# Recurrence of a hybrid decoder layer: products of two heads together, PSUM copies on VectorE, the fourth gate in another bank

## The chip, the cores and the metric

The kernel runs on one core of a Trainium2 chip. The metric is the device time of one execution in microseconds (us); the lower the better. The kernel before takes 1249.21 us, the median of three runs (1248.67 to 1249.44).

## What is computed

The reference is one decoder layer over 512 tokens of width 1024, in float32: a SwiGLU block, then two token mixers side by side (dilated attention, and a gated linear recurrence), a gated merge of the two, an output product, and a second SwiGLU block, with norms between. The change touches the recurrence and the merge gates. Cut to what matters:

```python
xc = causal_conv_width4(xr) + conv_b                       # xr = u @ w_in[:, xr columns]
gate_x = sigmoid(xh @ w_x + b_x); gate_a = sigmoid(xh @ w_a + b_a)   # per head of 256 channels, 4 heads
log_a = -8 * gate_a * softplus(-a_param)
h[t]  = exp(log_a)[t] * h[t-1] + sqrt(1 - exp(2*log_a))[t] * (gate_x * xc)[t]
rec   = h * gelu(yr)                                       # yr = u @ w_in[:, yr columns]
merged = sigmoid(gl0) * attn_d + sigmoid(gl1) * (rec @ w_rec_branch)  # gl = u @ w_in[:, gl columns]
```

## The kernel before, in words

Activations lie with channels on the 128 partitions and the 512 tokens along the free axis. A float32 product is made of three TensorE products of rounded parts: every operand is split into a high part (a ScalarE copy, line 263) and a low part (a VectorE subtraction, line 264), and `mm3` (lines 275 to 278) adds high by high, high by low and low by high into one PSUM bank. A product of one 128-channel block with the whole width (`gemm`, line 291) is thus 8 times 3 = 24 matmuls. The PSUM's eight banks are given out in two rings: `acc_ps` (line 266) with five banks, for the large products, and `aux_ps` (line 269) with three.

Weights arrive in one stream in the order of `stream_plan` (line 67), two blocks of 1024 columns to a load, into two raw buffers; `fetch` (line 223) splits a block into one of four `w8` buffers. The order in which an engine works is fixed when the program is built: a scheduler takes the instructions in the order of the Python text, except that `tc.high_priority(offset=...)` moves some of them ahead of it, a weight split by `AHEAD` = 100 places and a copy out of PSUM by `EVAC` = 200. What is not ready by the scheduler's own reckoning is passed over for what is. On the chip each engine then works through its list in that fixed order.

The recurrence (lines 981 to 1105) has four heads, `hd` = 0 to 3, of two channel blocks each. Its parts are:

- `conv(hd)`, line 1019: two products with `um`; ScalarE copies each PSUM result, with its tokens put in another order, into `xr` (line 1027); ScalarE and three VectorE steps make the convolution (lines 1029 to 1032) into a tile called `sig`; the result is split into `rec.hi` and `rec.lo` (line 1033).
- `branch(hd)`, line 1035: two products with `um`, each copied out by VectorE (line 1043) into a tile `ge`, of which there are four.
- `gates_of(hd)`, line 1047: four gate products of 6 matmuls each on the convolution's result, in four PSUM tiles that all come from the three banks of `aux_ps` (line 1054); ScalarE evacuates each with a sigmoid (line 1060) into a `gt` tile, of which there are six.
- `recur(hd)`, line 1064: some 14 ScalarE and 18 VectorE steps over the two blocks: tanh, exponential, square root and GELU on ScalarE (lines 1071 to 1086), products and the scan over time on VectorE (lines 1076 to 1091), and a split into `rec` at the end (line 1092). Its work tiles `th` and `r0` come from a ring of four.
- the merge gate of the recurrence: one product with `um` per block, and a sigmoid out of PSUM by ScalarE into `sig[:, c, :]` (line 1104). `GATE1` says which blocks stand behind which head: none behind head 0, two behind heads 1 and 2, four behind head 3.

The order before is: conv 0; then for each head branch(hd), conv(hd+1), gates and recurrence of hd, merge gates of `GATE1[hd]`. Behind it stands the product with `w_rec_branch` (line 1110), eight blocks whose 24 matmuls take `rec` block by block, so that the two blocks of head 3 are needed last. Each result is multiplied with the merge gate (line 1111).

Of the kernel before, what the change touches and what calls it, by code (L numbers as in the profile page):

```python
# [10 lines left out]
F32 = mybir.dt.float32  # L11
F32R = mybir.dt.float32r
AF = mybir.ActivationFunctionType
# [3 lines left out]
P = 128  # L17
T = 512
# [6 lines left out]
NH = 4  # L25
# [5 lines left out]
EVAC = 200  # L31
# [3 lines left out]
QKB = 6  # L35
CB = 6
GATE1 = ((), (0, 1), (2, 3), (4, 5, 6, 7))

# [26 lines left out]
def stream_plan():  # L67

    plan = []

    def down(n, a, half):
        for kk in range(part_blocks(a)):
            plan.append((("down", n, a, half, kk), 1024))

    def ffn(n):
        for ev in ffn_order(n):
            if ev[0] == "std":
                plan.append((("gate", n, ev[1]), 1024))
                plan.append((("up", n, ev[1]), 1024))
            elif ev[0] == "prep":  # L80
                plan.append((("gu", n, ev[1]), 2048))
            elif ev[0] == "down":
                down(n, *ev[1:])
            else:
                for half in ev[3]:
                    down(n, ev[2], half)
        for half in range(2):
            down(n, len(FF_PARTS) - 1, half)

    def values(g):  # L90
        for k in range(4):
            plan.append((("v", g, k), 1024))

    def qk(h):
        for g in range(NG):
            plan.append((("pair", g * 4 + h, 12 + g * 4 + h), 2048))

    ffn(1)
    del plan[:4]
    for k in range(KC):  # L100
        plan.insert(k, (("start", k), 512))
    for g in VALUES:
        values(g)
    for h in range(NH):
        qk(h)
    for c in range(0, KC, 2):
        plan.append((("pair", 52 + c, 53 + c), 2048))
    for m in range(KC):
        plan.append((("attn", m), 512))
    for h in range(-1, NH):  # L110
        if h >= 0:
            for c in (2 * h, 2 * h + 1):
                plan.append((("in", 44 + c), 1024))
        if h + 1 < NH:
            for c in (2 * h + 2, 2 * h + 3):
                plan.append((("in", 36 + c), 1024))
        if h < 0:
            continue
        plan.append((("lru", h), 1024))
        for c in GATE1[h]:  # L120
            plan.append((("in", 60 + c), 1024))
    for m in range(KC):
        plan.append((("rec", m), 1024))
    for half in range(2):
        for kk in range(4):
            plan.append((("out", half, kk), 1024))
    ffn(2)
    return plan
# [25 lines left out]
def hybrid_layer(ctx: ExitStack, tc: tile.TileContext, xT: bass.AP, xN: bass.AP, wst: bass.AP,  # L154
                 small: bass.AP, rows: bass.AP, consts: bass.AP, bias: bass.AP, out: bass.AP):
    nc = tc.nc
    DVE, ACT, PE = nc.vector, nc.scalar, nc.tensor
# [65 lines left out]
    def fetch(key, slot=None, ahead=0):  # L223

        with tc.high_priority(offset=ahead if slot else AHEAD):
            src = raw_of(key)
            w = src.shape[-1]
            t = slot() if slot else w8() if w > 512 else w4()
            split(t[:, 0, :w], t[:, 1, :w], src)
            return t[:, 0, :w], t[:, 1, :w]  # L230
# [35 lines left out]
    def acc_ps():  # L266
        return psum.tile([P, T], F32, name="acc", tag="acc", bufs=5)

    def aux_ps():
        return psum.tile([P, T], F32, name="aux", tag="aux", bufs=3)  # L270
# [20 lines left out]
    def gemm(ps, wt, x, sl=slice(0, T), n=None):  # L291
        n = n or x.n
        a, b = k128(wt[0], n), k128(wt[1], n)
        for k in range(n):
            mm3(ps, a[:, k, :], b[:, k, :], x.hi[k][:, sl], x.lo[k][:, sl], k == 0, k == n - 1)
# [446 lines left out]
    um = act_of(um_t[:2], um_t[2:])  # L742
# [12 lines left out]
    with ExitStack() as mx:  # L755
# [220 lines left out]
        for c in range(KC):  # L976
            ps = acc_ps()
# [3 lines left out]
    with ExitStack() as mx:  # L981
# [3 lines left out]
        sig = rpool.tile([P, KC, T], F32, name="sig")  # L985
        lpool_cm = tc.tile_pool(name="lru", bufs=1)
        lpool = lpool_cm.__enter__()
# [4 lines left out]
        o, w = SMALL["ap"]  # L992
# [20 lines left out]
        def ip(ap):  # L1013
            return ap.rearrange("q (i p) -> q p i", p=4)

        def pi(ap):
            return ap.rearrange("q (p i) -> q p i", p=4)

        def conv(hd):

            for c in (2 * hd, 2 * hd + 1):
                ps = acc_ps()
                gemm(ps, fetch(("in", 36 + c)), um)
                xr = lpool.tile([P, 3 + T], F32, name="xr", tag="xr", bufs=2)
                DVE.memset(xr[:, 0:3], 0.0)
                with tc.high_priority(offset=EVAC):
                    ACT.activation(ip(xr[:, 3:]), pi(ps), AF.Copy)
                xc = sig[:, c, :]
                ACT.activation(xc, xr[:, 3:], AF.Identity, bias=col("cb", c), scale=col("cw", 3 * 8 + c))
                for t in (2, 1, 0):  # L1030
                    DVE.scalar_tensor_tensor(xc, xr[:, t:t + T], col("cw", t * 8 + c), xc,
                                             op0=ALU.mult, op1=ALU.add)
                split(rec.hi[c], rec.lo[c], xc)

        def branch(hd):

            gel = []
            for c in (2 * hd, 2 * hd + 1):
                ps = acc_ps()
                gemm(ps, fetch(("in", 44 + c)), um)  # L1040
                ge = lpool.tile([P, T], F32, name="ge", tag="ge", bufs=4)
                with tc.high_priority(offset=EVAC):
                    DVE.tensor_copy(ge, ps)
                gel.append(ge)
            return gel

        def gates_of(hd):
            wh, wl = fetch(("lru", hd))
            a_ = wh.rearrange("p (w i c) -> p w i c", w=2, i=2)
            b_ = wl.rearrange("p (w i c) -> p w i c", w=2, i=2)  # L1050
            gs = {}
            for w, bn in ((1, "ba"), (0, "bx")):
                for j in range(2):
                    ps = aux_ps()
                    for i in range(2):
                        js = slice(j * P, (j + 1) * P)
                        mm3(ps, a_[:, w, i, js], b_[:, w, i, js], rec.hi[2 * hd + i], rec.lo[2 * hd + i],
                            i == 0, i == 1)
                    g = lpool.tile([P, T], F32, name="gt", tag="gt", bufs=6)
                    ACT.activation(g, ps, AF.Sigmoid, bias=col(bn, 2 * hd + j))  # L1060
                    gs[w, j] = g
            return [gs[1, j] for j in range(2)], [gs[0, j] for j in range(2)]

        def recur(hd, gel, gas, gxs):

            cs = (2 * hd, 2 * hd + 1)
            ths, rs = [tmp("th") for _ in cs], [tmp("r0") for _ in cs]
            for c, th, ga in zip(cs, ths, gas):  # L1070
                ACT.activation(th, ga, AF.Tanh, scale=sp4[:, c:c + 1])
            for c, r0, ga in zip(cs, rs, gas):
                ACT.activation(r0, ga, AF.Exp, scale=sp8[:, c:c + 1])
            for r0, th, ga in zip(rs, ths, gas):
                ACT.activation(r0, r0, AF.Copy, bias=0.5, scale=0.5)
                DVE.scalar_tensor_tensor(ga, th, 1.0, r0, op0=ALU.add, op1=ALU.mult)
                DVE.scalar_tensor_tensor(r0, ga, 2.0, r0, op0=ALU.subtract, op1=ALU.mult)
                DVE.tensor_mul(ga, th, r0)
            for c, gx in zip(cs, gxs):
                DVE.tensor_mul(gx, gx, sig[:, c, :])  # L1080
            for th in ths:
                ACT.activation(th, th, AF.Sqrt)
            for ga in gas:
                ACT.activation(ga, ga, AF.Copy, bias=1.0, scale=2.0)
            for ge in gel:
                ACT.activation(ge, ge, AF.Gelu_apprx_tanh)
            for c, r0, th, ga, gx, ge in zip(cs, rs, ths, gas, gxs, gel):
                DVE.scalar_tensor_tensor(th, th, -2.0, r0, op0=ALU.mult, op1=ALU.mult)
                DVE.tensor_mul(gx, gx, th)
                DVE.tensor_tensor_scan(th, ga, gx, 0.0, op0=ALU.mult, op1=ALU.add)  # L1090
                DVE.tensor_mul(pi(ge), ip(th), pi(ge))
                split(rec.hi[c], rec.lo[c], ge)

        conv(0)
        for hd in range(NH):
            gel = branch(hd)
            if hd + 1 < NH:
                conv(hd + 1)
            gas, gxs = gates_of(hd)
            recur(hd, gel, gas, gxs)  # L1100
            for c in GATE1[hd]:
                ps = acc_ps()
                gemm(ps, fetch(("in", 60 + c)), um)
                ACT.activation(sig[:, c, :], ps, AF.Sigmoid)
        lpool_cm.__exit__(None, None, None)

        mg = act_big("mg")
        for c in range(KC):
            ps = acc_ps()
# [145 lines left out]
```

## Time and profile before

| | |
|---|---|
| median of three runs | 1249.21 us |
| the profiled execution | 1251.04 us |
| its span | 1249.3 us |
| recurrence, from its first product to the first product with `w_rec_branch` | 645.2 to 802.1 us of the span |
| load of one 1024 KB pair of weight blocks, issue to landing | 4.8 us |

The profiled execution's span is what the engines' records cover; the rest of its time lies around it. In the rows below, PE is TensorE, PEld its weight loads, DVE VectorE, ACT ScalarE and SP the queue that issues the weight loads. A row of the timeline has the start and the length in microseconds, the engine, the line, the operation, what it writes and reads, and in brackets how long the engine stood idle before it and what it waited for. Neighbouring instructions of one kind are merged into a row, with their count. A matmul's row is longer (0.39 us) than the distance to the next one, because matmuls overlap.

### The profile page before, as it was taken

Reading aid. Unit: us, or ns where it says so; the run is one execution under the profiler, and the core shown is the slowest. Engines: PE = TensorE matmul, PEld = TensorE weight load, DVE = VectorE, ACT = ScalarE, POOL = GpSimd, SP = SyncE. Lnnn points to the kernel's source line nnn. Section 1 sums busy time; section 2 is a strip of 40 time slices with the busy share of each in tenths; the row PEclk is TensorE's granted clock in tenths of the full one; section 3 lists DMA queues with packets and bytes.
Section 4 is the critical chain, followed back from the end, with each engine's and each line's share of the span. In section 5 each row is a group of like instructions: output and inputs, shape, how many; then the busy total and the mean of one; then the engine's idle time right before and its main releaser. Section 6 shows DMA issues by size and latency. Waiting matters only on the chain.

```text
span 1249.3 us, 18949 instructions
## 1 busy us (share of the span) xinstructions
PE 1235.0 (99%) x7712; PEld 1117.5 (89%) x7712; DVE 911.3 (73%) x1427; ACT 670.5 (54%) x1105; POOL 26.1 (2%) x51
## 2 busy tenths in 40 slices
PE   9999999999999999999999999999999999999997
PEld 7899999999878899999987787888899999999985
DVE  6996777786577588888565877754795867777755
ACT  6655444455355365666546979634564544445432
POOL 0000000000002000000000000000100000000000
PEclk9999999999999999999999999999999999999999
DMA  6212222234424222222342122224451322222241
GB/s 241 102 68 102 102 102 103 103 133 171 172 97 144 87 91 102 77 97 82 111 160 102 68 101 102 101 101 168 135 169 68 136 102 102 102 102 74 103 178 67
DMA packets 27527, 141.37 MB, mean 113 GB/s; under 512 B 3120, under 2 KB 6320, under 8 KB 13360
## 3 DMA queue, kind: packets, MB, share of 16 engines
q1 hardware_dynamic: 20160, 122.86, 27.3%
q0 software_dynamic: 7280, 17.30, 4.1%
q8 instruction: 60, 0.98, 0.3%
q14 instruction: 27, 0.22, 0.1%
HBM read 129.67 MB, written 6.29 MB: 109 GB/s over the span
## 4 chain that ended last, share of the span: by engine, by line
PE 90%; DVE 5%; ACT 4%; DMA 1%; issue 1%; SPq 0%; DVEq 0%; ACTq 0%
PE acc L585 11%; PE acc L586 11%; PE acc L587 11%; PE acc L381 7%; PE acc L382 7%; PE acc L380 7%; PE acc L276 7%; PE acc L278 7%; PE acc L277 7%; PE aux L585 3%; PE aux L586 3%; PE aux L587 3%; PE acc L784 1%; PE acc L786 1%; PE acc L785 1%; DVE w L264 1%
## 5 line engine op out<-in xcount | busy, mean ns | idle before, releaser
L264 DVE TENSOR_TENSOR w<-raw,w 128x1024 fp32r<-128x1024 f32 (+1 forms) x241 | 257.9, 1074 | 115.8 <-ACT w L263 84.8
L263 ACT ACTIVATE w<-raw 128x1024 fp32r<-128x1024 f32 (+1 forms) x241 | 225.3, 938 | 181.5 <-DVE raw L566 60.4
L585 PE MATMUL acc<-big,w 128*128 128x256 f32 x880 | 251.2, 285 | 0.1
L586 PE MATMUL acc<-big,w 128*128 128x256 f32 x880 | 250.2, 284 | 0.0
L587 PE MATMUL acc<-big,w 128*128 128x256 f32 x880 | 249.9, 284 | 0.0
L585 PEld LDWEIGHTS acc<-big,w 128*128 128x128 f32 x880 | 168.7, 192 | 1.2 <-ACT c L592 0.3
L586 PEld LDWEIGHTS acc<-big,w 128*128 128x128 f32 x880 | 168.9, 192 | 0.6
L587 PEld LDWEIGHTS acc<-big,w 128*128 128x128 f32 x880 | 168.8, 192 | 0.0
L592 ACT ACTIVATE c<-acc 128x256 f32<-128x256 f32 x169 | 63.9, 378 | 79.7 <-PE acc L587 76.1
L380 PE MATMUL acc<-wd,act 128*128 128x512 f32 x256 | 99.9, 390 | 0.0
L381 PE MATMUL acc<-wd,act 128*128 128x512 f32 x256 | 99.9, 390 | 0.0
L382 PE MATMUL acc<-wd,act 128*128 128x512 f32 x256 | 99.5, 390 | 0.0
L585 PE MATMUL aux<-big,w 128*128 128x256 f32 x280 | 79.4, 283 | 0.0
L586 PE MATMUL aux<-big,w 128*128 128x256 f32 x280 | 79.3, 283 | 0.0
L587 PE MATMUL aux<-big,w 128*128 128x256 f32 x280 | 79.3, 283 | 0.0
L585 PE MATMUL acc<-tx,w 128*128 128x256 f32 x268 | 76.2, 284 | 0.0
L586 PE MATMUL acc<-tx,w 128*128 128x256 f32 x268 | 76.0, 283 | 0.0
L587 PE MATMUL acc<-tx,w 128*128 128x256 f32 x268 | 75.9, 283 | 0.0
L276 PE MATMUL acc<-big,w 128*128 128x512 f32 x192 | 74.8, 389 | 0.0
L278 PE MATMUL acc<-big,w 128*128 128x512 f32 x192 | 74.8, 389 | 0.0
L277 PE MATMUL acc<-big,w 128*128 128x512 f32 x192 | 74.8, 389 | 0.0
L264 DVE TENSOR_TENSOR w<-s,w 128x1024 fp32r<-128x1024 f32 x51 | 62.4, 1224 | 10.4 <-ACT w L263 10.3
(309 smaller groups left out, 2763.5 us busy)
## 6 DMA issues: line engine op xcount, KB each, us to landing
raw<-in_w SPq DMA_DIRECT2D x110, 1024.0 KB, 4.8
big<-act POOLq DMA_DIRECT2D x6, 512.0 KB, 4.3
gains<-in_rows POOLq DMA_DIRECT2D x5, 512.0 KB, 4.9
raw<-in_w SPq DMA_DIRECT2D x8, 256.0 KB, 5.1
h<-in_x SPq DMA_DIRECT2D x8, 256.0 KB, 5.2
h<-in_xn POOLq DMA_DIRECT2D x4, 512.0 KB, 7.2
kept_m<-h POOLq DMA_DIRECT2D x4, 512.0 KB, 2.9
h<-kept_m POOLq DMA_DIRECT2D x4, 512.0 KB, 5.9
```

What stands on the lines that cost most here:

```text
L263: ACT.activation(dh, src, AF.Copy)
L264: DVE.tensor_sub(dl, src, dh.bitcast(F32))
L276: PE.matmul(ps, wh, xh, start=first, stop=False)
L277: PE.matmul(ps, wh, xl, start=False, stop=False)
L278: PE.matmul(ps, wl, xh, start=False, stop=last)
L380: PE.matmul(ps, x.hi[k][:, bl], wh, start=k == 0, stop=False)
L381: PE.matmul(ps, x.hi[k][:, bl], wl, start=False, stop=False)
L382: PE.matmul(ps, x.lo[k][:, bl], wh, start=False, stop=k == x.n - 1)
L585: PE.matmul(ps, wh, xh, start=start and k == 0, stop=False, skip_group_check=True)
L586: PE.matmul(ps, wh, xl, start=False, stop=False, skip_group_check=True)
L587: PE.matmul(ps, wl, xh, start=False, stop=k == 3, skip_group_check=True)
L592: ACT.activation(c, ps, AF.Copy)
```

## The change

A hand-written order, `LRU_ORDER`, takes the place of the loop over heads, for the weight stream as for the program:

conv 0, branch 0, branch 1, conv 1, gates 0, conv 2, gates 1, merge gates of head 1, branch 2, branch 3, conv 3, gates 2, merge gates of head 2, gates 3, merge gates of head 3.

Here "gates" stands for the gate products and the recurrence behind them. Within it:

```diff
-                    ACT.activation(ip(xr[:, 3:]), pi(ps), AF.Copy)
+                    DVE.tensor_copy(ip(xr[:, 3:]), pi(ps))
...
-                ge = lpool.tile([P, T], F32, name="ge", tag="ge", bufs=4)
+                ge = lpool.tile([P, T], F32, name="ge", tag="ge", bufs=8)
...
+        def gelus(hds):
+            for hd in hds:
+                for ge in gels[hd]:
+                    ACT.activation(ge, ge, AF.Gelu_apprx_tanh)
+
+        def sigmoids():
+
+            while late:
+                c = late.pop(0)
+                ACT.activation(sig[:, c, :], sig[:, c, :], AF.Sigmoid)
+
+        def gate1(hd):
+            for c in GATE1[hd]:
+                ps = acc_ps()
+                gemm(ps, fetch(("in", 60 + c)), um)
+                with tc.high_priority(offset=EVAC):
+                    DVE.tensor_copy(sig[:, c, :], ps)
+                late.append(c)
...
+            sigmoids()
             for w, bn in ((1, "ba"), (0, "bx")):
                 for j in range(2):
-                    ps = aux_ps()
+                    ps = aux_ps() if w or not j else acc_ps()
...
-            for ge in gel:
-                ACT.activation(ge, ge, AF.Gelu_apprx_tanh)
...
+        for what, hd in LRU_ORDER:
+            if what == "gates":
+                recur(hd, gels.pop(hd), *gates_of(hd))
+            else:
+                {"conv": conv, "branch": branch, "gate1": gate1}[what](hd)
+                if what == "branch" and hd % 2:
+                    gelus((hd - 1, hd))
+        sigmoids()
```

So the four GELUs of two heads stand together behind their branch products; the convolution's input and the merge gates are copied out of PSUM by VectorE; the merge gates' sigmoids stand, on the copied tile, ahead of the next head's gate sigmoids, and those of head 3 at the very end; and the fourth gate product of each head goes to one of the five banks of `acc_ps`.

More of the change, by code (lines that the diff above doesn't have):

```diff
@@ L37 @@
 GATE1 = ((), (0, 1), (2, 3), (4, 5, 6, 7))
+LRU_ORDER = (("conv", 0), ("branch", 0), ("branch", 1), ("conv", 1), ("gates", 0), ("conv", 2), ("gates", 1),
+             ("gate1", 1), ("branch", 2), ("branch", 3), ("conv", 3), ("gates", 2), ("gate1", 2), ("gates", 3),
+             ("gate1", 3))
 def ffn_order(n):
@@ L109, in stream_plan @@
         plan.append((("attn", m), 512))
[L110 to L121, printed above, removed]
+    for what, h in LRU_ORDER:
+        if what == "gates":
+            plan.append((("lru", h), 1024))
+        else:
+            cs = GATE1[h] if what == "gate1" else (2 * h, 2 * h + 1)
+            o = {"conv": 36, "branch": 44, "gate1": 60}[what]
+            for c in cs:
+                plan.append((("in", o + c), 1024))
     for m in range(KC):
@@ L1033, in conv @@
                 split(rec.hi[c], rec.lo[c], xc)
+        gels, late = {}, []
         def branch(hd):
-            gel = []
+            gels[hd] = []
             for c in (2 * hd, 2 * hd + 1):
@@ L1040, in branch @@
                 gemm(ps, fetch(("in", 44 + c)), um)
-                ge = lpool.tile([P, T], F32, name="ge", tag="ge", bufs=4)
+                ge = lpool.tile([P, T], F32, name="ge", tag="ge", bufs=8)
                 with tc.high_priority(offset=EVAC):
                     DVE.tensor_copy(ge, ps)
-                gel.append(ge)
-            return gel
+                gels[hd].append(ge)
+        def gelus(hds):
[13 more added lines that the diff above has]
+                late.append(c)
         def gates_of(hd):
@@ L1092, in recur @@
                 split(rec.hi[c], rec.lo[c], ge)
[L1094 to L1104, printed above, removed]
+        for what, hd in LRU_ORDER:
+            if what == "gates":
+                recur(hd, gels.pop(hd), *gates_of(hd))
+            else:
+                {"conv": conv, "branch": branch, "gate1": gate1}[what](hd)
+                if what == "branch" and hd % 2:
+                    gelus((hd - 1, hd))
+        sigmoids()
         lpool_cm.__exit__(None, None, None)
```

## Prediction

> **What bounds the kernel now.** I first read the page for the engine that never rests.
>
> ```profile
> span 1249.3 us, 18949 instructions
> PE 1235.0 (99%) x7712; PEld 1117.5 (89%) x7712; DVE 911.3 (73%) x1427; ACT 670.5 (54%) x1105; POOL 26.1 (2%) x51
> ```
>
> TensorE is busy for 99% of the span; its whole idle time is 14 us. A change elsewhere gains only by closing a hole in its row. So the second view is the recurrence by itself, and the third the waits in it.
>
> ```profile
> 645.20:802.10 156.90, 153.67 (x674) 125.89 (x674) 114.99 (x148) 122.33 (x155) 0.00 (x0) 1.00 0.28 99
> ```
>
> ```profile
> PE aux L276 <- ACT gt L1060: 3.2, 4, 1.5
> DVE ge L1043 <- PE acc L278: 5.2, 2, 3.1
> ACT w L263 <- DMA raw<-in_w: 4.5, 1, 4.5
> ```
>
> The columns of the first are span, then busy time of PE, PEld, DVE, ACT. In 156.90 us TensorE is idle for 3.2 (156.90 less 153.67), and the waits name one cause: four times it stands before a gate product until a gate sigmoid (line 1060) is done. The granted clock is 1.00. Weights from memory made ScalarE wait once, at the stage's start, and TensorE never. The timeline shows each wait.
>
> ```profile
> 682.19 0.39 PE L277 MATMUL acc<-big,w 128*128 128x512 f32 x1
> 683.33 0.50 PE L276 MATMUL aux<-rec,w 128*128 128x512 f32 x1 [0.75 <-ACT gt L1060]
> ...
> 710.90 0.39 PE L276 MATMUL acc<-big,w 128*128 128x512 f32 x1
> 712.82 0.51 PE L276 MATMUL aux<-rec,w 128*128 128x512 f32 x1 [1.54 <-ACT gt L1060]
> ...
> 750.40 0.39 PE L277 MATMUL acc<-big,w 128*128 128x512 f32 x1
> 751.54 0.50 PE L276 MATMUL aux<-rec,w 128*128 128x512 f32 x1 [0.76 <-ACT gt L1060]
> ...
> 778.24 0.39 PE L278 MATMUL aux<-rec,w 128*128 128x512 f32 x1
> 778.80 0.50 PE L276 MATMUL aux<-rec,w 128*128 128x512 f32 x1 [0.18 <-ACT gt L1060]
> ```
>
> It is the same matmul each time, the first of a head's fourth gate product: three banks, four tiles, and the fourth has to wait until the first is read. The reader is late because of what ScalarE has in front of it; for head 2:
>
> ```profile
> 746.85 1.08 ACT L1027 ACTIVATE xr<-acc 128x512 f32<-128x512 f32 x1
> ...
> 749.51 1.28 ACT L1060 ACT_TABLE_LOAD   x1
> 750.80 1.27 ACT L1060 ACTIVATE gt<-aux,sm 128x512 f32<-128x512 f32 x2
> ```
>
> A copy from PSUM, two more steps and a table load come first. The sigmoid starts at 750.80, and TensorE goes on at 751.54, when the first of the two has ended. The gate products themselves had begun at 746.09:
>
> ```profile
> 746.09 0.39 PE L276 MATMUL aux<-rec,w 128*128 128x512 f32 x1
> ...
> 749.94 0.39 PE L278 MATMUL aux<-rec,w 128*128 128x512 f32 x1
> ```
>
> These are the 18 matmuls of three gates, 3.85 us from first to last start: a matmul every 3.85 / 17 = 0.227 us.
>
> **The change, part by part.**
>
> *Fourth gate in another bank.* Start to start, the four stalls are 1.14, 1.92, 1.14 and 0.56 us, so over the pitch of 0.227 0.91 + 1.69 + 0.91 + 0.33 = 3.84 us. The stalled matmul itself is longer than the others, 0.50 for 0.39, which I take as 0.11 more, four times 0.44. Sum: **4.3 us** that TensorE loses in the stage, and the most that this edit can return. I take all of it: the new bank is one of five, and the tile five products earlier was copied out long ago, a product being 24 times 0.227 = 5.44 us. Its own reader may come late, since it is next needed five products, some 27 us, further on. What this adds is therefore nothing; if that cover is gone the gain is (below).
>
> *Is anything else late at TensorE in the new order?* Gates need a convolution that is split. The convolution products that ended where head 2's gates began, at 746.09, were split by 753.97:
>
> ```profile
> 753.29 0.68 DVE L264 TENSOR_TENSOR rec<-sig,rec 128x512 fp32r<-128x512 f32 x1
> ```
>
> That is 7.9 us. In the new order the closest pairs, conv 1 to gates 1 and conv 3 to gates 3, have a gates part (5.44) and two products (10.88) between them, 16.3 us. It costs nothing. The weight loads keep number and size, 28 blocks in the stage in pairs; only their order changes, so the waiting row above is my bound for SP's queue: zero.
>
> *Copies moved to VectorE, table loads saved.*
>
> ```profile
> L1027 ACT ACTIVATE xr<-acc 128x512 f32<-128x512 f32 x8 | 8.7, 1086 | 12.0 <-PE acc L278 12.0
> L1091 DVE TENSOR_TENSOR ge<-th,ge 128x512 f32<-128x512 f32 x8 | 8.5, 1070 | 0.0
> L1104 ACT ACT_TABLE_LOAD x6 | 7.7, 1283 | 0.1
> L1043 DVE COPY ge<-acc 128x512 f32<-128x512 f32 x8 | 5.5, 682 | 5.2 <-PE acc L278 5.2
> L1104 ACT ACTIVATE sig<-acc 128x512 f32<-128x512 f32 x8 | 4.8, 595 | 0.1
> ```
>
> VectorE gains eight merge-gate copies at 0.68 (the row of line 1043 is the same copy), 5.5 us, and eight copies with reordered tokens. These no row shows; the straight copy's 0.68 and ScalarE's 1.09 for the same views bound them. I take 1.07, as line 1091, which reads the same reordered view: 8.6 us. VectorE goes from 115.0 to 129 of then 152.6 us. ScalarE loses 8.7 us of copies, and most of the six table loads of line 1104 (7.7 us), and some for GELU; the sigmoids stay. All of it lies beside TensorE, except at the end of the stage.
>
> *The tail, where it is tight.* Before, a branch pair (10.9 us) stood between gates 2 and gates 3. It has gone to the front, so both last recurrences must end sooner: rec is read right behind the last merge gate. Let T be the start of gates 2. Gates 2, two products, gates 3, four products make 8 x 5.44 = 43.5 us; block 7's low part is wanted at the 23rd matmul behind, at T + 43.5 + 22 x 0.227 = **T + 48.5**. From before:
>
> ```profile
> 770.34 1.08 DVE L1091 TENSOR_TENSOR ge<-th,ge 128x512 f32<-128x512 f32 x1
> ...
> 784.91 0.69 DVE L1076 SCALAR_TENSOR_TENSOR gt<-th,r 128x512 f32<-128x512 f32 x1 [2.48 <-ACT r L1075]
> ...
> 800.79 0.68 DVE L264 TENSOR_TENSOR rec<-ge,rec 128x512 fp32r<-128x512 f32 x1
> ```
>
> ```profile
> 780.40 0.72 ACT L1071 ACTIVATE th<-gt,sp 128x512 f32<-128x512 f32 x1
> ```
>
> Head 2 frees its second `th` tile 771.42 - 746.09 = 25.3 us after its gates start, and head 3's second tanh wants that tile. From that tanh to head 3's first product before: 784.91 - 780.40 = 4.5. From there to the last split: 801.47 - 784.91 = 16.6, VectorE without a hole. To this come some three merge-gate copies, 3 x 0.60 (copies follow each other closer than their length) = 1.8. Sum T + 48.2. Head 2's first sigmoid came 4.7 us after its gates' start (750.80 - 746.09), 1.1 of them ScalarE's xr copy, which goes: T + 47.1. **To spare: 1.4 us.** Before it was 5.6: the low part was ready at 801.47, its matmul came at 807.04:
>
> ```profile
> 807.04 0.39 PE L277 MATMUL acc<-rec,w 128*128 128x512 f32 x1
> ```
>
> So the tail costs nothing by the sum, but it is next in line.
>
> [...] What does a table switch cost on the tail's chain?
>
> ```profile
> 686.02 0.73 ACT L1071 ACTIVATE th<-gt,sp 128x512 f32<-128x512 f32 x1
> 686.76 1.28 ACT L1073 ACT_TABLE_LOAD   x1
> 688.05 1.34 ACT L1073 ACTIVATE r<-gt,sp 128x512 f32<-128x512 f32 x2
> ```
>
> The tanh ends at 686.75 and the exponential starts at 688.05: 1.30 us in all. [...]
>
> **The sum.** The profiled execution, 1251.04 us with a span of 1249.3, would take 1246.7; from its span 1245.0. The three timed runs have the median 1249.21, so the time is 1249.21 - 4.3 = 1244.9, and 1245.0 with a tenth left for the new bank's own start.
>
> **Rivals.**
>
> 1. *The merge sigmoids break up the tail.* They are ready early, and a ScalarE that is idle may run them between tanh, exponential and root, as it did before. One such insertion on head 3's chain is two loads and a sigmoid, 1.28 + 0.60 + 1.28 = 3.2 us: T + 50.3, TensorE 1.8 late, 1246.7. Two insertions: 5.0 late, 1249.9. For it: six loads for eight sigmoids before. Against: VectorE, not ScalarE, set the pace between 784.91 and 801.47.
>
> 2. *Slower: copies at the head of VectorE's queue.* The four merge-gate copies behind gates 3 stand in a fixed order among head 3's products; where one is placed too early, VectorE waits for TensorE and the scan behind it waits with it. Line 1043 waited so twice, 5.2 us in all, 2.6 on average. If all four wait so: T + 47.1 + 10.4 = T + 57.5, TensorE 9.0 late, **1253.9**. It loses from 1.4 + 4.3 = 5.7 us of waiting on. Against: a weight split or the next product can mostly be put in front.
>
> 3. *The change doesn't do what it says*: the fourth bank isn't free in time, since its reader waits for a `gt` tile of the head before (six tiles, four a head). Then the hole stays: 1249.2. Against: five banks, 27 us.
>
> [...]
>
> **Chances.** Forecast 0.62 (1244.4 to 1246.0, allowing 0.5 for the runs' own spread and up to 1 us of tail); rival 1 0.16, half of it still over the bound; rival 2 0.12; rival 3 0.08; rival 4 0.02. About 0.2% (2.5 us) is what a measurement of this kernel can tell from no change: faster means below 1246.7, slower above 1251.7. Faster 0.62 + 0.08 = 0.70; same 0.08 + 0.08 + 0.02 = 0.18 ; slower 0.12. The range goes from 1244.2 up to where rivals 1 and 3 end, 1249.9, and leaves out rival 2.
>
> **What would show it.** Right: the wait row of line 276 for line 1060 is gone, the stage from the first conv product to the first `rec` product lasts 152.6 us, and that product's blocks 6 and 7 follow at 0.227. Tail wrong: a hole in TensorE at the 19th to 23rd matmul of the first rec product, with VectorE's or ScalarE's split into `rec` as the releaser; then rivals 1 and 2 are told apart by whether VectorE waited for ScalarE or for TensorE before it. Rival 3: the hole is still at the fourth gate, now on an acc tile. The forecast fails as a whole if a convolution's split, a weight split or a copy out of PSUM turns up as a releaser of TensorE elsewhere in the stage.

## The result, and the profile after

| | before | after |
|---|---|---|
| median, 14 runs each | 1249.28 us (1248.27 to 1250.89) | 1251.83 us (1249.87 to 1253.42) |
| ratio, 95% interval | | 1.0019 (1.0012 to 1.0026) |
| the profiled execution | 1251.04 us | 1251.77 us |
| first product of the recurrence to first product with `w_rec_branch` | 156.82 us | 158.78 us |

The kernel became 2.5 us slower; 4.2 us less was forecast. From the page of after, the span, the engines and the one group of instructions that answers to the stalls of before:

```profile
span 1250.0 us, 18953 instructions
...
PE 1234.3 (99%) x7712; PEld 1117.3 (89%) x7712; DVE 921.0 (74%) x1443; ACT 657.8 (53%) x1092; POOL 26.2 (2%) x51
...
L278 PE MATMUL acc<-big,w 128*128 128x512 f32 x192 | 75.6, 394 | 4.3 <-DVE w L264 4.3
```

The wait of line 276 for line 1060 is gone. In its place stands one that before did not have: TensorE waits 4.3 us in products with `um`, for VectorE (line 264) to make the low part of a weight. TensorE's timeline in after has it twice:

```profile
714.53 0.39 PE L277 MATMUL acc<-big,w 128*128 128x512 f32 x1
716.01 0.50 PE L278 MATMUL acc<-big,w 128*128 128x512 f32 x1 [1.09 <-DVE w L264]
...
732.23 0.39 PE L277 MATMUL acc<-big,w 128*128 128x512 f32 x1
735.79 0.50 PE L278 MATMUL acc<-big,w 128*128 128x512 f32 x1 [3.17 <-DVE w L264]
...
736.98 0.63 PE L276 MATMUL acc<-big,w 128*128 128x512 f32 x1
737.40 0.63 PE L277 MATMUL acc<-big,w 128*128 128x512 f32 x1
...
807.13 0.39 PE L276 MATMUL acc<-rec,w 128*128 128x512 f32 x1
807.88 0.50 PE L277 MATMUL acc<-rec,w 128*128 128x512 f32 x1 [0.36 <-DVE rec L264]
```

It is the third matmul of a product that stands, the first that takes the weight's low part: the first product's high parts are there, so two matmuls go ahead and the third waits. The first time it is head 1's second merge gate, the second time the first product of branch 3. Behind the second wait the matmuls follow at 0.42 us and not at 0.227 (736.98 to 737.40). The last pair is the tail: the low part of block 7 in `rec` is late by a little.

Over the pitch of 0.227 the starts are late by 716.01 - 714.53 - 0.227 = 1.25, by 735.79 - 732.23 - 0.227 = 3.33 and by 0.52 (807.88 - 807.13 - 0.227); each stalled matmul is 0.11 longer; and eight matmuls at 0.42 cost 8 x 0.195 = 1.56. Sum: 1.36 + 3.44 + 0.63 + 1.56 = **7.0 us lost in after, 4.3 in before**: 2.7 more, where the medians differ by 2.55. (The two profiled executions differ by only 0.73: in before the stage begins at 645.24 us of the span, in after at 643.59, behind code that is the same.) The slow clock seems not to have come in every execution: in three of the 14 runs of after the mean granted clock was 0.998, as in most runs of the kernels without such a stretch, in the other eleven 0.995 to 0.997, and those three are the fastest, 1249.87 to 1250.47 us.

Where the weight stood: first ScalarE's timeline of after, with the high parts of branch 3's two blocks, then VectorE's, with the low part of the first.

```profile
722.50 1.99 ACT L263 ACTIVATE w<-raw 128x1024 fp32r<-128x1024 f32 x2
```

```profile
730.34 2.34 DVE L1109 TENSOR_TENSOR_SCAN th<-gt 128x512 f32<-128x512 f32 x2
732.59 2.02 DVE L1110 TENSOR_TENSOR ge<-th,ge 128x512 f32<-128x512 f32 x2
734.51 1.22 DVE L264 TENSOR_TENSOR w<-raw,w 128x1024 fp32r<-128x1024 f32 x1
```

ScalarE begins at 722.50; VectorE, with the same raw block, begins at 734.51, **12 us later**, right behind the scan and the last product (line 1110) of head 1's recurrence. It did not wait for anything: it worked without a hole through the stretch, in the order of its list. The view of stretches shows that, columns as in the prediction; before and then after, from 698 to 741 us:

```profile
698.00:741.00 43.00, 41.46 (x183) 34.01 (x182) 36.20 (x47) 34.94 (x45) 0.00 (x0) 1.00 0.30 106
```

```profile
698.00:741.00 43.00, 38.74 (x163) 31.27 (x162) 42.58 (x56) 34.20 (x46) 0.00 (x0) 0.96 0.17 56
645.20:802.10 156.90, 152.64 (x665) 125.59 (x664) 118.76 (x157) 106.47 (x139) 0.00 (x0) 0.99 0.25 88
```

VectorE is busy for 42.58 of 43.00 us in after (36.20 before). Over the whole stage (third row, after) the same engine shows 118.76 of 156.90, three quarters: a mean in which the full stretch can't be seen.

### The profile page after: what moved, and what is told of

Its sections match the earlier page's. It is cut to its first block, busy times and chain, and to the rows that moved or that the text cites. A ratio compares the mean times of both kernels' runs of the same rounds, so it can differ in the third digit from the quotient of the medians.

```text
span 1250.0 us, 18953 instructions
## 1 busy us (share of the span) xinstructions
PE 1234.3 (99%) x7712; PEld 1117.3 (89%) x7712; DVE 921.0 (74%) x1443; ACT 657.8 (53%) x1092; POOL 26.2 (2%) x51
## 4 chain that ended last, share of the span: by engine, by line
PE 87%; DVE 6%; ACT 5%; issue 1%; DMA 0%; SPq 0%; DVEq 0%; ACTq 0%
PE acc L585 11%; PE acc L586 11%; PE acc L587 11%; PE acc L381 7%; PE acc L382 7%; PE acc L380 7%; PE acc L276 6%; PE acc L278 6%; PE acc L277 6%; PE aux L585 3%; PE aux L586 3%; PE aux L587 3%; PE acc L784 1%; PE acc L786 1%; PE acc L785 1%
```

## The experiments

Two theories stood against each other. **A**: the order. Gates 0 and gates 1 are now close, so the recurrences of heads 0 and 1 and the convolution of head 2 fall on VectorE one behind the other, and a weight's split, put ahead by a fixed number of places, ends up behind a recurrence. **B**: the copies. VectorE has been given 14 us of work out of PSUM and has no room for the splits. None of the nine kernels leaves out any of the computation; the copies that f4 and f5 add write a tile onto itself.

**e1, the bank alone**, on the kernel before:

```diff
-                    ps = aux_ps()
+                    ps = aux_ps() if w or not j else acc_ps()
```

> The kernel before with one part of the change: the fourth gate product of each head goes to a bank of the large ring. Nothing else is touched. My theory (the bank alone returns the 4.3 us that TensorE lost before the fourth gates, and the loss of the changed kernel comes from elsewhere): 1245.0, the four waits of TensorE for the gate sigmoid gone, no new one. Rival (the bank edit itself brings the new waits): 1249 or more, with TensorE waiting for a weight split.

Measured: 1245.12 us, ratio 0.9964 (0.9951 to 0.9978). The stage, in the view of stretches:

```profile
645.00:810.00 165.00, 165.00 (x730) 136.73 (x729) 121.13 (x156) 125.44 (x160) 0.00 (x0) 1.00 0.28 97
```

TensorE 165.00 of 165.00: no hole is left. From the first product at 643.53 to the first with `w_rec_branch` at 795.86 are 152.33 us. One line of the change brings all that was forecast for the whole.

**e2, after in the old order**, copies and sigmoids as in after:

```diff
+LRU_ORDER = (("conv", 0), ("branch", 0), ("conv", 1), ("gates", 0), ("branch", 1), ("conv", 2), ("gates", 1),
+             ("gate1", 1), ("branch", 2), ("conv", 3), ("gates", 2), ("gate1", 2), ("branch", 3), ("gates", 3),
...
-                if what == "branch" and hd % 2:
-                    gelus((hd - 1, hd))
+                if what == "branch":
+                    gelus((hd,))
```

> The changed kernel with the heads in the order of before (each head's branch products in front of the next head's convolution, GELUs of one head together); bank, VectorE's copies and late sigmoids stay as changed. Theory A (the order packs the recurrences of heads 0 and 1 with convolution 2 into a stretch where VectorE has no room): VectorE has holes between every two recurrences again, TensorE waits for no weight split, about 1245. Rival B (the copies given to VectorE are too much in whatever order): a wait of TensorE for a low-part split of over 1 us remains, 1247 to 1251.

Measured: 1245.14 us, 0.9961 (0.9948 to 0.9973). The same view:

```profile
698.00:741.00 43.00, 43.00 (x192) 35.62 (x191) 39.90 (x52) 32.73 (x42) 0.00 (x0) 1.00 0.29 103
645.00:810.00 165.00, 165.00 (x730) 136.72 (x729) 131.70 (x172) 120.16 (x152) 0.00 (x0) 1.00 0.28 98
```

VectorE has 10.6 us more to do than in e1 (131.70 against 121.13), and it costs nothing. The copies alone are not the cause.

**e3, after with the convolution's copy back on ScalarE**:

```diff
-                    DVE.tensor_copy(ip(xr[:, 3:]), pi(ps))
+                    ACT.activation(ip(xr[:, 3:]), pi(ps), AF.Copy)
```

> The changed kernel with the convolution's copy out of PSUM back on ScalarE (line 1027); order, bank and late sigmoids as changed. Theory A: the order is still too dense, VectorE gets back two copies of 1.0 us in the stretch, so the second wait of TensorE for a low-part split shrinks from 3.2 to about 1 us and the slow clock behind it goes: about 1247 to 1248. Rival B (the copies are the cause): no wait for a split is left, 1245.

Measured: 1247.45 us, 0.9979 (0.997 to 0.9988). No wait for a weight is left in the profiled execution, though the order is that of after; what is left is the tail, in TensorE's timeline:

```profile
800.91 0.50 PE L276 MATMUL acc<-rec,w 128*128 128x512 f32 x1 [0.24 <-ACT rec L263]
...
802.58 0.50 PE L277 MATMUL acc<-rec,w 128*128 128x512 f32 x1 [1.16 <-DVE rec L264]
```

So the order alone is not the cause either; the sign is B's, the number A's. The profiled execution, at 1246.40 us, was the fastest of eleven; what made the median 1.05 us longer is not seen.

**e4, after with the stage's weight splits 200 places ahead, not 100**:

```diff
+    lead = [AHEAD]
...
-        with tc.high_priority(offset=ahead if slot else AHEAD):
+        with tc.high_priority(offset=ahead if slot else lead[0]):
```

with `lead[0] = 200` ahead of the recurrence's loop and `AHEAD` again behind it (its lines below stand two further on than in after).

> The changed kernel with weight splits of the recurrence stage moved 200 places ahead instead of 100; the work and its order otherwise as changed. Theory A in its sharper form (VectorE's list puts the split behind a whole recurrence): the split is done early, TensorE waits for no split, VectorE is still busy without a hole for some 40 us, the tail keeps its half microsecond: about 1245.5. Rival (VectorE lacks the capacity, so the wait only moves to another releaser, a convolution's split or a copy out of PSUM): still over 2 us of TensorE waits in the same stretch, 1248 or more.

Measured: 1246.3 us, 0.9971 (0.9959 to 0.9982). The view of stretches, then a split from ScalarE's and from VectorE's timeline:

```profile
698.00:741.00 43.00, 43.00 (x192) 35.62 (x191) 42.02 (x57) 37.15 (x50) 0.00 (x0) 1.00 0.28 97
```

```profile
727.97 1.04 ACT L265 ACTIVATE w<-raw 128x1024 fp32r<-128x1024 f32 x1
```

```profile
729.16 1.22 DVE L266 TENSOR_TENSOR w<-raw,w 128x1024 fp32r<-128x1024 f32 x1
```

The order of after, all its copies, VectorE busy for 42.02 of 43.00 us, and TensorE without a hole. In the split shown the low part follows the high part by 1.2 us. VectorE isn't short of time, so B as a matter of room falls as well: what counts is the place of the split in the list. 0.5 us in the tail is left.

**f1, after with both copies off VectorE** (order and bank alone): e3's edit and

```diff
-                with tc.high_priority(offset=EVAC):
-                    DVE.tensor_copy(sig[:, c, :], ps)
-                late.append(c)
+                ACT.activation(sig[:, c, :], ps, AF.Sigmoid)
```

> The changed kernel without VectorE's new copies: the convolution's copy and the merge gate's sigmoid come out of PSUM on ScalarE again, as before; new order, GELUs together and the bank stay. Theory A as the runs so far leave it (the dense order and the copies together fill VectorE; the dense tail is late by the order alone): no wait for a weight split in the crowded stretch; at the first product with w_rec_branch a hole of 1 to 2 us stays, since a branch pair is gone from between the last two heads: about 1247. Rival (the tail is late because merge-gate copies stand in VectorE's list among the last head's steps): no hole there either, 1245.

Measured: 1246.51 us, 0.9969 (0.9956 to 0.9981). No wait at all; the tail's low part, VectorE's row and then TensorE's:

```profile
801.87 0.69 DVE L264 TENSOR_TENSOR rec<-ge,rec 128x512 fp32r<-128x512 f32 x1
```

```profile
802.62 0.50 PE L277 MATMUL acc<-rec,w 128*128 128x512 f32 x1
```

It ends at 802.56, and its matmul starts at 802.62: on time by nothing. That the order by itself makes the tail 1 to 2 us late fell; in the new order the tail hole comes when the merge-gate copies, with their late sigmoids, are there too. The stage lasts 152.32 us, in e1 152.33; the median's 1.4 us over e1 lie outside it. In the profiled executions the stage begins 1.7 us later than in e1 (645.24 against 643.53), behind the same code; over all kernels of this study that start differs by 2.5 us (642.86 to 645.39), and why stays open. The two ratios' intervals overlap.

The four corners together, medians in us:

| | old order | new order |
|---|---|---|
| copies on ScalarE | e1: 1245.12 | f1: 1246.51 |
| copies on VectorE | e2: 1245.14 | after: 1251.83 |

Each alone costs 0 to 1.4 us, the two together 6.7; by the ratios to before, 0 to 0.6 and 6.9. The new order includes the GELUs of two heads together, and the lower row the late sigmoids of the merge gates.

**f2, after with the merge gates' sigmoid back on ScalarE** (the second edit of f1 alone).

> The changed kernel with the merge gate's sigmoid straight out of PSUM on ScalarE, as before; the convolution's copies stay on VectorE, order and bank as changed. Theory A: in the crowded stretch VectorE is rid of two merge-gate copies of 0.6 us, so the second wait of TensorE for a low-part split shrinks by about 1.2 us, from 3.2 to 2, and the first by nothing: 1248 to 1250. Rival (only the convolution's copies matter): waits as in the changed kernel, 1251.8. Rival (any relief is enough): no wait for a split, 1245 to 1246.

Measured: 1246.53 us, 0.9972 (0.9962 to 0.9983): better than expected. The first wait stays (1.07 us, at 717.80). The second is gone altogether, not smaller by the copies taken out, and VectorE's timeline says why:

```profile
727.94 1.23 DVE L264 TENSOR_TENSOR w<-raw,w 128x1024 fp32r<-128x1024 f32 x1
729.07 1.30 DVE L1105 SCALAR_TENSOR_TENSOR th<-th,r 128x512 f32<-128x512 f32 x2
```

The split now stands within the recurrence, ahead of the step `th` (in after line 1107), and no longer behind the scan and all. Here the effect is not in proportion to the work; it goes by places.

**f3, after with branch 2 between conv 2 and gates 1**:

```diff
-("gates", 0), ("conv", 2), ("gates", 1),
-             ("gate1", 1), ("branch", 2), ("branch", 3), ("conv", 3),
+("gates", 0), ("conv", 2), ("branch", 2),
+             ("gates", 1), ("gate1", 1), ("branch", 3), ("conv", 3),
```

> The changed kernel with one step of the order moved: branch 2 stands between convolution 2 and gates 1 instead of behind the merge gates of head 1, so that the first two recurrences are 27 us apart instead of 16. All VectorE copies stay. Theory A (density is the cause): no wait for a split in the stretch, the tail's half microsecond stays: 1245.5 to 1246. Rival (the copies fill VectorE in any spacing): the waits stay, 1248 or more.

Measured: 1246.77 us, 0.9976 (0.9966 to 0.9985). With gates 0 and 1 two products further apart the long wait and the slow clock are gone (granted 1.00 from 698 to 741 us, 0.96 in after); a short wait for a weight is left, and 0.7 us in the tail, so the time is a little above the 1245.5 to 1246 expected:

```profile
720.21 0.50 PE L278 MATMUL acc<-big,w 128*128 128x512 f32 x1 [0.58 <-DVE w L264]
```

**f4, after with two more copies** on VectorE behind head 1's scan, ahead of the late split:

```diff
+                if hd == 1:
+                    DVE.tensor_copy(th, th)
```

> The changed kernel with two VectorE copies of a tile onto itself (0.6 us each) in the recurrence of head 1, straight ahead of the late weight split in VectorE's list; results are the same. Theory A: the second wait of TensorE grows from 3.2 to 4.4 us, one for one. Theory on the clock (a wait of this length makes TensorE run at half clock for some microseconds behind it, in some executions and not in others while the wait is near 3 us, in all when it is longer): another 0.5 to 1 us, 1253.3 to 1254.5 with less spread between runs. Rival (VectorE's backlog is not what TensorE waits for): no change, 1251.8.

Measured: 1252.03 us, 1.0019 (1.001 to 1.0028), as after. From VectorE's timeline:

```profile
732.42 0.75 DVE L1111 COPY th<-th 128x512 f32<-128x512 f32 x2
...
735.02 1.23 DVE L264 TENSOR_TENSOR w<-raw,w 128x1024 fp32r<-128x1024 f32 x1
```

Such a copy takes only 0.33 us (the two begin at 732.42, the next step at 733.07), the split came 0.5 later (735.02 against 734.51), and the wait stayed at 3.17, as TensorE reached it later too. Too small a dose: it settles nothing on whether added work lengthens the wait one for one.

**f5, three such copies for each block**, six in all.

> The changed kernel with six VectorE copies of a tile onto itself in the recurrence of head 1 (0.33 us each, as the run with two of them showed), ahead of the late weight split in VectorE's list; results are the same. Theory on the clock (what counts is that TensorE stood still for about 3 us or more, and the half clock then lasts a fixed time): TensorE's wait there grows to about 5 us, the matmuls behind it follow each other by 0.43 us for about 3.4 us as before, no longer: some 2 us slower than the changed kernel, 1253.5 to 1254. Rival (the slow stretch grows with the wait): 0.43 us for 5 us or more, 1255 or more. Rival (the scheduler's list makes up for it with other matmuls): the wait stays near 3 us and the time near 1252.

Measured: 1254.74 us, 1.0038 (1.0024 to 1.0052), between what the theory and its first rival gave. The list came out differently, and instead of one wait of 5 us there are three shorter ones. TensorE's waits, and the two stretches behind them:

```profile
714.74 0.79 PE L278 MATMUL acc<-big,w 128*128 128x512 f32 x1 [3.87 <-DVE w L264]
...
739.65 0.50 PE L276 MATMUL acc<-big,w 128*128 128x512 f32 x1 [1.25 <-ACT w L263]
...
741.36 0.50 PE L278 MATMUL acc<-big,w 128*128 128x512 f32 x1 [0.98 <-DVE w L264]
```

```profile
715.20:718.20 3.00, 3.00 (x8) 2.32 (x8) 3.00 (x5) 2.98 (x5) 0.00 (x0) 0.51 0.22 27
742.20:745.40 3.20, 3.20 (x9) 2.48 (x8) 3.13 (x5) 0.00 (x0) 0.00 (x0) 0.50 0.37 95
```

The slow clock came twice, each time for about 3.4 us (matmuls start over 0.3 us apart from 714.74 to 718.25 and from 741.93 to 745.58), behind a wait of 3.87 and behind two of 1.25 and 0.98. From a wait of 3.17 us in after to one of 3.87 here it did not grow.

## Why the prediction failed, step by step

*Fourth gate in another bank*: right, in size too. 4.3 us were to come back and a stage of 152.6 us to remain; e1 has 152.33 us, no hole, and 1245.12 us, where 1245.0 was forecast.

*Copies and table loads*: the copies were right in price, the table loads in part. The groups of after, from 645 to 808 us:

```profile
L1027 DVE COPY xr<-acc 128x512 f32<-128x512 f32 x8 | 8.7, 1083 | 8.5 <-PE acc L278 8.5
...
L1064 DVE COPY sig<-acc 128x512 f32<-128x512 f32 x8 | 5.5, 684 | 0.0
...
L1057 ACT ACT_TABLE_LOAD x5 | 6.4, 1283 | 0.1
```

The copy with reordered tokens takes 1.083 us, for the 1.07 taken. Of the merge gates' six table loads only one went, where most were to go; with those for GELU the stage has 18 loads where before had 23.

*"All of it lies beside TensorE, except at the end of the stage"*: **this is the step that failed.** It went by a mean, 129 of 152.6 us. The question of what else could be late was asked of the convolution's splits, and of the weights' way from memory, and answered rightly for both; it was not asked of the weights' own splits, which need VectorE for each block and stand in its list at a place given as a number of instructions. That 100 places are enough was taken over from the order of before. With convolution, gates and recurrence closer together, and the copies ahead of it all, 100 places no longer reach over a recurrence: the low part is 12 us behind the high part. It costs 1.36 + 3.44 us and then 1.56 for the slow clock, 6.4 us where 4.3 were gained. e4 shows that the place decides: VectorE is as full there, and the waits are gone. e2 and f1 show that the order and the copies are needed together. How the scheduler came to each place is argued from its rule, not shown.

*The tail*: next in line, as said, but the sum was too short. Gates 2 start at T = 758.85, and the last split ends at 807.83, T + 49.0; T + 47.1 was forecast, with T + 48.5 as the limit. The rows of after, TensorE, then VectorE, then ScalarE:

```profile
758.85 0.39 PE L276 MATMUL aux<-rec,w 128*128 128x512 f32 x1
```

```profile
781.86 2.03 DVE L1110 TENSOR_TENSOR ge<-th,ge 128x512 f32<-128x512 f32 x2
...
791.09 1.29 DVE L1097 SCALAR_TENSOR_TENSOR gt<-th,r 128x512 f32<-128x512 f32 x2 [1.35 <-ACT r L1096]
...
807.15 0.68 DVE L264 TENSOR_TENSOR rec<-ge,rec 128x512 fp32r<-128x512 f32 x1
```

```profile
783.92 0.63 ACT L263 ACTIVATE rec<-ge 128x512 fp32r<-128x512 f32 x1 [0.35 <-DVE ge L1110]
784.46 0.67 ACT L1081 ACTIVATE gt<-aux,sm 128x512 f32<-128x512 f32 x1
785.03 0.68 ACT L1081 ACTIVATE gt<-acc,sm 128x512 f32<-128x512 f32 x1
785.60 1.33 ACT L1092 ACTIVATE th<-gt,sp 128x512 f32<-128x512 f32 x2
786.82 1.06 ACT L263 ACTIVATE w<-raw 128x1024 fp32r<-128x1024 f32 x1
787.90 1.28 ACT L1094 ACT_TABLE_LOAD   x1
789.20 1.34 ACT L1094 ACTIVATE r<-gt,sp 128x512 f32<-128x512 f32 x2
...
792.55 1.28 ACT L1057 ACT_TABLE_LOAD   x1
793.84 0.63 ACT L1057 ACTIVATE sig<-sig 128x512 f32<-128x512 f32 x1
794.49 1.28 ACT L1103 ACT_TABLE_LOAD   x1
```

The `th` tile is free at 783.89 (781.86 + 2.03), T + 25.0 and not 24.2. The second tanh doesn't start then but at about 786.2, as two of head 3's gate sigmoids stand on ScalarE behind the split of head 2's `rec`, which waits for VectorE: 2.3 us that the sum did not have. From there to the first product are 4.9 us (4.5 forecast), and 16.7 to the end (18.4 forecast: the three merge-gate copies are there, but three weight splits and not four as in before). 0.8 + 2.3 + 0.4 - 1.7 = 1.8 us. It cost 0.63 us.

*Rivals*: the second (copies in VectorE's list ahead of the tail) was near in kind, as f1 and f2 without the merge-gate copies have no such hole and e3, e4 and after do; but VectorE doesn't stand for TensorE there, and the price was 0.5 to 2 us, not 9. As f1 and f2 lack the late sigmoids too, these runs don't tell the copies from the sigmoids. The first came in after, without its price: a merge sigmoid with two table loads stands between head 3's exponential and its root (792.55 to 795.77 in the rows above), but VectorE works without a hole from 791.09 to 807.83 and never waits for it. The third did not come. The 0.02 of the chances under rival 4 stand for a table switch that costs more than its load, and no run shows one: in after the weight split ends at 787.88 and the exponential starts at 789.20, 1.32 us for the whole switch, 1.28 of them the load. The slower outcome came by a mechanism that was not among the rivals, only among the signs that would make the forecast fail: a weight split as the releaser.

## What to carry to other kernels

Before work is moved to an engine with "room", find the stretch where it is fullest, and list every consumer that depends on a small step of that engine there. A full stretch by itself cost nothing in e4; but in such a stretch a step that stands late in the list has no hole to catch up in, and a weight's split of 1.2 us that stood 12 us late cost more than the 14 us of copies did in the old order. A lead given as a number of instructions is a lead in time only for the order in which it was tuned: a change of order has to look at it again. And test the parts alone, since here one line gave the whole gain, over 4 us, and the rest, nearly free in either half, gave it back and more.

## What the runs showed of the hardware

The slow clock was not expected. In after, the stretch behind the wait of 3.17 us, then the one behind that, in the view of stretches (the third column from the end is the granted clock):

```profile
736.60:740.00 3.40, 3.40 (x10) 2.63 (x9) 3.40 (x5) 0.41 (x1) 0.00 (x0) 0.50 0.11 19
740.00:745.00 5.00, 5.00 (x23) 4.14 (x22) 1.66 (x4) 1.54 (x2) 0.00 (x0) 1.00 0.95 369
```

The clock was 0.50 for about 3.4 us though TensorE was busy all the time, and 1.00 again after it. In the profiled executions it came in the recurrence after waits of 3.17 and 3.87 us, and in f5 also after shorter ones, 1.25 and 0.98 us (2.2 in two parts), that ended 1.7 us apart, but not after the single wait of 1.54 us in before nor after one of 1.09 in after: the clock was 1.00 over the 3.4 us from 712.80 and from 716.00. Where the limit lies no run here tells. A long wait of TensorE can thus be dearer than its length: in the profiled execution 3.44 us cost 5.0.
